# A row maximum on one core: the first block's store moved behind the loads, the load lists retuned, and the last row loaded and reduced in two chained halves

## Chip, cores, metric

One Trainium2 chip, one core of it. The metric is the device time of one execution in microseconds (us); for each kernel the median of several executions is given. The span of a profile is about 1.8 us shorter than the device time of the same execution.

## The reference

```python
x = randn(32, 512, 1024) as float32       # 16384 rows of 1024
return np.max(x, axis=-1)                 # (32, 512) float32
```

Flattened, there are 16384 rows, 128 for each of the 128 partitions. "A row" below means one row in every partition: 128 x 1024 elements, 512 KB. The kernel handles 128 of them.

## The kernel before

Loads go out on the sync queue into a ring of 46 rows; VectorE reduces each load in one instruction. Loads shrink towards the end, so that little is left to reduce once the last one lands. The results leave in two stores on the scalar queue, one for each block: 112 rows (57 KB) and 16 rows (8 KB).

```python
BLOCKS = [
    [14, 14, 12, 11, 9, 8, 8, 7, 6, 5, 4, 4, 4, 3, 3],
    [2, 2, 2, 2, 2, 1, 1, 1, 1, 1, 1],
]
RING = 46
# ... (cut: views of x and out, pools)
    at = first = 0
    for loads in BLOCKS:
        S = sum(loads)
        xb = xf[first * P:(first + S) * P, :].rearrange("(p i) d -> p i d", p=P)
        b = 0
        for g in loads:
            if at + g > RING:
                at = 0
            xc = ring[:, at:at + g, :]
            nc.sync.dma_start(out=xc, in_=xb[:, b:b + g, :])
            nc.vector.reduce_max(out=res[:, first + b:first + b + g], in_=xc, axis=X)
            at += g
            b += g
        dst = bass.AP(tensor=of.tensor, offset=of.offset + first * P, ap=[[S, P], [1, S]])
        nc.scalar.dma_start(out=dst, in_=res[:, first:first + S])
        first += S
```

## Time and profile before

| | before |
|---|---|
| median (range) | 165.06 us (165.01 to 165.14) |
| span of the profile | 163.32 us |
| VectorE (DVE) busy | 138.5 us, 85% |
| load queue's packets, share of the 16 DMA engines | 96.4% |
| first load landed, last load landed | 20.09, 159.46 |
| last reduction | 159.67 to 160.88 |
| small store, issue to landing | 160.91 to 162.33 |
| end | 163.32 |

Times in the lower four rows are from the span's start. A load or store has "landed" when the last of its sixteen semaphore increments is in the trace. The chain, the waits and the windows of this profile stand in the prediction.

### The profile page before, as it was taken

The numbers are of one execution on the slowest core, as the hardware profiler recorded it, in microseconds if no ns is written. First come the engines' busy times: TensorE is split into PE (matmuls) and PEld (weight loads), VectorE is DVE, ScalarE is ACT, GpSimd is POOL, SyncE is SP. The second block draws the span as 40 slices with busy tenths as digits, with TensorE's granted clock in tenths as the row PEclk, the third lists the DMA queues.
The fourth block names the chain that finished last, engine by engine and source line by source line (L and its number), as shares of the span: only waits on it lengthen the run. The fifth ranks groups of instructions, "written<-read, shape, count | busy, mean of one in ns | idle before, by whom it ended". The sixth has DMA issues, their size and how long they took to land.

```text
span 163.3 us, 109 instructions
## 1 busy us (share of the span) xinstructions
DVE 138.5 (85%) x26; POOL 0.2 (0%) x4
## 2 busy tenths in 40 slices
DVE  0000099969999999999999999999999999999994
POOL 0000000000000000000000000000000000000000
DMA  6999999998899897999989999999999999999980
GB/s 225 449 449 449 449 449 449 449 417 385 385 409 522 353 530 321 433 433 441 473 385 473 425 449 400 434 395 451 413 425 433 429 414 418 425 421 419 404 357 2
DMA packets 4032, 67.18 MB, mean 411 GB/s; under 512 B 704, under 2 KB 704, under 8 KB 1472
## 3 DMA queue, kind: packets, MB, share of 16 engines
q1 hardware_dynamic: 3744, 67.11, 96.4%
q10 hardware_dynamic: 288, 0.07, 0.2%
HBM read 67.11 MB, written 0.07 MB: 411 GB/s over the span
## 4 chain that ended last, share of the span: by engine, by line
DMA 57%; DVE 40%; DVEq 1%; SPq 0%; issue 0%
DMA ring<-in_x_dram 57%; DVE res L50 40%; DVEq L82 1%; SPq L49 0%
## 5 line engine op out<-in xcount | busy, mean ns | idle before, releaser
L50 DVE TENSOR_REDUCE res<-ring 128x1 f32<-128x1024 f32 (+11 forms) x26 | 138.5, 5396 | 22.4 <-DMA ring<-in_x_dram 22.4
L71 POOL MEMSET const-bfloat16-1.0<- 128x1 bf16 x1 | 0.1, 101 | 0.0
L71 POOL MEMSET const-uint8-127<- 128x1 uint8 x1 | 0.1, 101 | 0.0
L71 POOL MEMSET const-float32-0.0<- 128x1 f32 x1 | 0.1, 98 | 0.2 <-issue 0.2
L71 POOL MEMSET const-float32-1.0<- 128x1 f32 x1 | 0.1, 98 | 0.0
## 6 DMA issues: line engine op xcount, KB each, us to landing
ring<-in_x_dram SPq DMA_DIRECT2D x2, 7168.0 KB, 27.6
ring<-in_x_dram SPq DMA_DIRECT2D x2, 4096.0 KB, 31.6
ring<-in_x_dram SPq DMA_DIRECT2D x1, 6144.0 KB, 49.9
ring<-in_x_dram SPq DMA_DIRECT2D x3, 2048.0 KB, 36.8
ring<-in_x_dram SPq DMA_DIRECT2D x1, 5632.0 KB, 29.7
ring<-in_x_dram SPq DMA_DIRECT2D x5, 1024.0 KB, 24.6
ring<-in_x_dram SPq DMA_DIRECT2D x1, 4608.0 KB, 23.7
ring<-in_x_dram SPq DMA_DIRECT2D x1, 3584.0 KB, 38.4
```

The source lines that it names most:

```text
L50: nc.vector.reduce_max(out=res[:, first + b:first + b + g], in_=xc, axis=X)
L71: nc = _bacc.Bacc("TRN2", target_bir_lowering=False, num_devices=1)
L82: with _tile.TileContext(nc) as tc:
```

## The change

The intent: keep the 57 KB store out of the way of the loads, and have less to reduce after the last landing, by cutting the last row in two. The first half's maximum is written into the element just in front of the second half, so that the second reduction, over 513 elements, takes it in. The load lists are retuned, the ring gives up one row. The intent is read from the code.

```diff
-    [14, 14, 12, 11, 9, 8, 8, 7, 6, 5, 4, 4, 4, 3, 3],
-    [2, 2, 2, 2, 2, 1, 1, 1, 1, 1, 1],
+    [14, 13, 12, 11, 9, 8, 8, 7, 6, 5, 5, 4, 4, 3, 3],
+    [2, 2, 2, 1, 1, 1, 1, 1, 1, 1, 1, 1],
-RING = 46
+RING = 45
     # ... (cut: `H`, `PAD` and the tile `tail`; the loop is as before, but does not store; `reduce` is its last reduction)
-        nc.scalar.dma_start(out=dst, in_=res[:, first:first + S])
+    half = ring[:, at, :H]
+    nc.sync.dma_start(out=half, in_=xb[:, b, :H])
+    nc.sync.dma_start(out=tail[:, PAD:], in_=xb[:, b, H:])
+    nc.vector.reduce_max(out=tail[:, PAD - 1:PAD], in_=half, axis=X)
+    nc.vector.reduce_max(out=res[:, I - 1:], in_=tail[:, PAD - 1:], axis=X)
+
+    store = nc.scalar.dma_start(out=views[0][0], in_=views[0][1])
+    tc.add_manual_dep(store.ins, reduce.ins.name, SYNC, reason="behind the loads")
+    nc.scalar.dma_start(out=views[1][0], in_=views[1][1])
```

More of the change, by code (lines that the diff above doesn't have):

```diff
@@ L13 @@
 BLOCKS = [
-    [14, 14, 12, 11, 9, 8, 8, 7, 6, 5, 4, 4, 4, 3, 3],
-    [2, 2, 2, 2, 2, 1, 1, 1, 1, 1, 1],
-]
-RING = 46
+    [14, 13, 12, 11, 9, 8, 8, 7, 6, 5, 5, 4, 4, 3, 3],
+    [2, 2, 2, 1, 1, 1, 1, 1, 1, 1, 1, 1],
+]
+RING = 45
+SYNC = mybir.DependencyInfo(mybir.DependencyClass.Sync, mybir.DependencyReason.DATA)
 @with_exitstack
@@ L32 @@
     N, D = xf.shape
+    H = D // 2
     I = N // P
@@ L38 @@
     res = once.tile([P, I], F32)
+    PAD = 16
+    tail = once.tile([P, PAD + H], F32)
     at = first = 0
+    views = []
     for loads in BLOCKS:
-        S = sum(loads)
+        S = sum(loads) + (loads is BLOCKS[-1])
         xb = xf[first * P:(first + S) * P, :].rearrange("(p i) d -> p i d", p=P)
+        dst = bass.AP(tensor=of.tensor, offset=of.offset + first * P, ap=[[S, P], [1, S]])
+        views.append((dst, res[:, first:first + S]))
         b = 0
-        for g in loads:
-            if at + g > RING:
+        for n in loads:
+            if at + n > RING:
                 at = 0
-            xc = ring[:, at:at + g, :]
-            nc.sync.dma_start(out=xc, in_=xb[:, b:b + g, :])
-            nc.vector.reduce_max(out=res[:, first + b:first + b + g], in_=xc, axis=X)
-            at += g
-            b += g
-        dst = bass.AP(tensor=of.tensor, offset=of.offset + first * P, ap=[[S, P], [1, S]])
-        nc.scalar.dma_start(out=dst, in_=res[:, first:first + S])
+            xc = ring[:, at:at + n, :]
+            nc.sync.dma_start(out=xc, in_=xb[:, b:b + n, :])
+            reduce = nc.vector.reduce_max(out=res[:, first + b:first + b + n], in_=xc, axis=X)
+            at += n
+            b += n
         first += S
     assert first == I
+    if at + 1 > RING:
+        at = 0
+    half = ring[:, at, :H]
[6 more added lines that the diff above has]
+    nc.scalar.dma_start(out=views[1][0], in_=views[1][1])
 _INS = ['x']
```

## The prediction

> **What bounds the kernel now.** I read the page first: VectorE (DVE) is 85% busy, the load queue's packets take 96.4% of the DMA engines' time. Neither is clearly the bound, so I went to the chain that ended last, in order of time:
>
> ```profile
> 0.73 0.37 SPq L49
> 1.15 35.88 DMA ring<-in_x_dram
> 37.05 58.02 DVE res L50 x5
> 95.08 36.77 DMA ring<-in_x_dram
> 131.87 19.94 DMA ring<-in_x_dram
> 151.84 7.92 DVE res L50 x6
> 159.75 1.13 DVEq L82
> ```
>
> Columns: start, length, what. The loads carry the end up to 151.81 us; from there seven reductions run back to back, x6 plus the last one (1.13 us, shown under the exit). Then comes the small store, issued at 160.91, and the exit at 163.3.
>
> The waits say how close the two streams are:
>
> ```profile
> DVE res L50 <- DMA ring<-in_x_dram: 22.4, 4, 20.1
> ...
> SPq L49 <- DVE res L50: 77.6, 7, 15.1
> SPq L49 <- DMA ring<-in_x_dram: 56.5, 10, 18.0
> ...
> SPq L49 <- DMA out_dram<-res: 5.0, 1, 5.0
> ```
>
> Columns: total us, times, longest. DVE waits only four times, 20.1 us of it for the first load. The sync queue's long waits look alarming but harm nothing if the DMA engines never run dry. I tested that with the windows view, cut at the moments (the trace's semaphore increments) when one load had landed and the next began to count:
>
> ```profile
> 131.85:135.55 3.70, 3.70 (x2) 0.00 (x0) 1.00 1.01 425
> ...
> 144.21:146.70 2.49, 2.49 (x2) 0.00 (x0) 1.00 1.02 424
> 146.70:149.33 2.63, 2.63 (x2) 0.00 (x0) 1.00 1.02 421
> 149.33:151.81 2.48, 2.31 (x2) 0.00 (x0) 1.00 0.99 413
> 151.81:153.09 1.28, 1.25 (x1) 0.00 (x0) 1.00 1.02 406
> ```
>
> The sixth column is the share of DMA engines busy, about 1.0 up to the last load, as in every earlier stretch. So landings are spaced by transfer alone: 16.94 us for 14 rows (20.09 to 37.03), 14.53 for 12, 9.71 for 8, 4.90 for 4, 3.69 for 3, 2.49 for 2, 1.28 for 1. A line through these is **1.2045 us per row plus 0.08 us per load**. One interval is off: 2.63 in place of 2.49, exactly where the 57 KB store's packets run (146.4 to 149.0). The store costs the load stream 0.14 us. The last load lands at 159.46.
>
> VectorE is a little faster per row:
>
> ```profile
> L50 DVE TENSOR_REDUCE res<-ring 128x14 f32<-128x14336 f32 x2 | 30.2, 15086 | 22.0 <-DMA ring<-in_x_dram 22.0
> L50 DVE TENSOR_REDUCE res<-ring 128x8 f32<-128x8192 f32 x2 | 17.4, 8681 | 0.2 <-DMA ring<-in_x_dram 0.2
> ...
> L50 DVE TENSOR_REDUCE res<-ring 128x2 f32<-128x2048 f32 x5 | 11.2, 2279 | 0.2 <-DMA ring<-in_x_dram 0.2
> ...
> L50 DVE TENSOR_REDUCE res<-ring 128x1 f32<-128x1024 f32 x6 | 6.8, 1208 | 0.0
> ```
>
> From 2279 and 1208 ns one row costs 1.07 us. Starts of back-to-back reductions are closer than the durations, since one begins about 0.08 us before the other ends: 1.127 us for 1 row, 2.194 for 2, 3.26 for 3, 4.327 for 4, 5.393 for 5. Thus a row costs 1.067 and an instruction 0.06. The two streams run nearly level: DVE works off the backlog of a big load over the shrinking ones. At the end it is still behind: the last load is complete at 159.46 and its reduction starts at 159.67.
>
> **What the Trainium skill says.** "DMA: Bandwidth & Descriptors", section "Specifications", gives a fabric ceiling of 435 GB/s; my slope is 524,288 B / 1.2045 us = 435 GB/s, so the trace agrees and the loads cannot go faster per byte. The same page, "Issuing engines are not separate DMA queues", says that DMAs of all issuers interleave on the same 16 engines; the 2.63 us interval is that. "VectorE: DVE Perf Modes", section "The perf-mode tier table", gives tensor_reduce only the 1x mode; 1.067 us per 1024 elements (0.96 per ns) agrees, so there is no quicker form. The same page, "The DRAIN you can't avoid", says a same-engine read-after-write needs its semaphore: the chained halves pay one exposed completion. The trace before has no such pair, so I estimate it.
>
> **The change, part by part.** I used the landings above and the two start-to-start rules. A reduction starts at the later of its landing (plus 0.02) and its predecessor's slot.
>
> 1. *Load sizes.* The first 13 loads hold 106 rows in both kernels (before 14,14,12,11,9,8,8,7,6,5,4,4,4; after 14,13,12,11,9,8,8,7,6,5,5,4,4). So load 13 lands at the same 131.85. The ring shrinks by a row, yet each load is still issued with others in flight: load 4 waits for the first reduction (35.2) while loads 2 and 3 last until 50.4; load 6 waits for the third (63.3) while load 5 lasts to 74.6. A reuse wait for the completion of the load eight back is also early: the last half may go at 150.5, nine us before it lands. No starvation.
>
> 2. *Load stream at the end.* 22 rows remain in both. Before: 13 loads and the store's 0.14. After: 16 loads (two halves), no store among them. Three loads more cost 3 x 0.08 = 0.24; the store gives back 0.14. Last landing about 159.46 + 0.10 = 159.56.
>
> 3. *VectorE.* Before, reduction 13 starts at 131.91. After, its predecessor ends its slot at 131.76, so it starts on the landing, 131.87. Then: 4.327 + 2 x 3.26 + 3 x 2.194 + 9 x 1.127 = 27.57, so the first half starts at 159.44, though it has been there since about 158.9. VectorE, not the load, bounds the end. A half of 512 elements lasts 1.208 - 0.533 = 0.675, ending 160.11. The second reads the first's result: it starts only after that, plus 0.03 (the release that the trace shows from VectorE to the scalar queue, 160.879 to 160.912), and lasts 0.676: end 160.82. Before: 160.88. Gain **0.06 us**. Broken up: without the store VectorE would not have stood 0.19 us before the load at 151.81 plus small lag elsewhere (about 0.3 in all); the extra instructions cost about 0.06 each for two splits, and two chained halves cost 0.675 + 0.03 + 0.676 = 1.38 against 1.21 for one row, a loss of 0.17. The halving is a loss where VectorE is late.
>
> 4. *Stores.* The big store is issued at 159.53, once the last whole row is reduced. With no load before it, I take the small store's 1.42 us from issue to landing (160.91 to 162.33) plus a few tenths: lands by 161.5. Its issue occupies the scalar queue 0.38 us, to 159.9. The small store goes at 160.85 and lands at about 162.27. Nothing is added behind.
>
> 5. *Exit.* The sync engine waits for eight completion semaphores in four pairs, in fixed order; in the trace these steps are 0.07 us apart (162.39, 162.46, 162.53) once the first is released. In the built programs the small store's semaphore sits in the first pair before and in the third after. Two steps, 0.13 us, then pass before the landing: gain **0.13 us**.
>
> Sum: 0.06 + 0.13 = 0.19 us. 165.07 - 0.19 = **164.88 us**.
>
> **The rivals.** (a) *The end follows the load, as the change intends*: the second half would start at 159.58 and end at 160.26, for 164.3 us. For: the halves are smaller than a row. Against: the row sums leave VectorE 0.5 us late, and chaining serializes. (b) *The big store lies at the end*: if its short runs of 448 B take as long to land as before (142.87 to 149.51, 6.6 us), the end would be at 166.2 and the time near 168.9, slower by over 2%. For: that number. Against: its packets first ran 3.5 us after issue, behind queued loads, and took 25 ns each, eight per engine; with the queue empty that shrinks to tenths of a us. (c) *Small descriptors cost more than the line says*: 2 KB runs or nine one-row loads slowing the stream by 0.1 each where VectorE catches up: at most 1 us, 165.9. Against: six one-row loads ran at 1.25 to 1.29.
>
> **Range and chances.** Runs spread by 0.13 us. My terms are each below 0.3, their errors mostly independent; about 0.3 us around 164.88, widened downward for (a) and upward for (c) and for another chip: 164.4 to 165.3. A 2% change is 3.3 us, over ten times every gain I find: faster 0.01; slower 0.015, for (b); within 2% 0.975.
>
> **What would show it.** Right: the big store's packets stand after the last load; no 2.63 us interval; last half landed near 159.55; VectorE without a wait after 131.9 and two reductions of 0.68 us separated by about 0.03; small store issued near 160.85; exit shorter by 0.13. Wrong: VectorE waiting for a half (rival a), the exit waiting for the big store (b), or one-row landings spaced over 1.35 us (c). A wait in the chained pair of some tenths rather than 0.03 would put the time level with before.

## The result

| | median | lowest to highest | ratio to before, 95% interval |
|---|---|---|---|
| before, 6 runs | 165.06 us | 165.01 to 165.14 | |
| changed, 6 runs | 165.02 us | 164.87 to 165.17 | 0.9997, 0.9984 to 1.001 |

A ratio here is the mean time of one kernel's fast runs over that of the other's of the same rounds, so not quite the ratio of the medians quoted. The two kernels are the same within 2%, and the interval holds 1. The predicted 164.88 is 0.14 us low; the measured time lies in the predicted range of 164.4 to 165.3.

The profile of the changed kernel was taken of its slowest run (165.17), and its first load landed at 20.29 instead of 20.09: everything in it stands 0.2 us later from the start. Keep that in mind for each time read from it. The chain that ended last, start, length and what:

```profile
63.94 30.30 DMA ring<-in_x_dram
94.24 0.02 issue
94.27 65.48 DVE res L58 x21
159.75 0.60 DVE tail L69
160.35 0.02 issue
160.38 0.69 DVE res L70
```

Before, the loads carried the end up to 151.81. Now the view stays on VectorE from 94.27 on: 21 reductions, then the halves (L69 and L70).

The view shows a wait only where the engine stood idle. Back to back, a reduction starts about 0.08 us before the one in front of it ends, so a late landing can hold VectorE up unseen. Call the earliest start that the predecessor allows the slot; the prediction's start-to-start times give it (1.127 us after the start of a one-row reduction, 4.327 after one of four rows). In the changed kernel the last start that a landing set is that of the 13th reduction: it began at 132.09, on its landing (132.07), where its slot was 127.69 + 4.327 = 132.02. From there on VectorE alone sets the starts: 27.57 us pass to the first half (132.09 to 159.66), exactly the sum that the prediction worked out. But it does not stay far behind the loads. Over the nine single rows, which land every 1.28 us and take 1.127, its lateness shrinks from 1.33 us to 0.09. The windows between landings:

```profile
144.42:146.91 2.49, 2.49 (x2) 0.00 (x0) 1.00 1.00 410
146.91:148.19 1.28, 1.28 (x2) 0.00 (x0) 1.00 1.02 406
...
158.44:159.11 0.67, 0.67 (x2) 0.00 (x0) 1.00 0.65 232
```

Two rows land in 2.49 us, one in 1.28, half a row in 0.67. The interval of 2.63 us, in which the big store ran, is gone. The DMA issues of the big store (KB, us from issue to landing), of the kernel before and then of the changed one:

```profile
out_dram<-res ACTq DMA_DIRECT2D x1, 56.0 KB, 6.6
```

```profile
out_dram<-res ACTq DMA_DIRECT2D x1, 56.0 KB, 1.6
```

It takes 1.6 us where nothing is queued in front of it. The end of the changed kernel in order of time (start, length, engine, line, what):

```profile
159.66 0.68 DVE L69 TENSOR_REDUCE tail<-ring 128x1 f32<-128x512 f32 x1
159.78 0.38 ACTq L73 DMA_DIRECT2D out_dram<-res  x1
160.38 0.69 DVE L70 TENSOR_REDUCE res<-tail 128x1 f32<-128x513 f32 x1
161.10 0.34 ACTq L75 DMA_DIRECT2D out_dram<-res  x1
```

The first half had landed at 159.11 and is taken up at 159.66: VectorE is 0.55 us late. Nearly all of this comes from the last whole row, which landed at 158.44, was taken up at 158.53 and holds its slot for 1.127 us. The second half landed at 159.75 and has to wait until 160.38 for the first's result. So the halves are reduced one after the other, both after their data.

To compare traces whose first load landed at different times, two measures are used below. **A** is the end of the last reduction minus the landing of the first load; it holds all that the load stream and VectorE do. **B** is the end of the span minus the end of the last reduction; it holds the small store and the exit, which is what the engines still do once that store has landed.

| kernel | A | B | median |
|---|---|---|---|
| before | 140.79 | 2.44 | 165.06 |
| changed | 140.77 | 2.33 | 165.02 |

A is unchanged within 0.02 us, B is 0.11 shorter. Over all thirteen traces the first load landed between 19.99 and 20.29; that alone moves a single run by as much as any part of this change.

### The profile page after: what moved, and what is told of

Read it like the earlier page. It is cut to its first block, busy times and chain, and to the rows that moved or that the text cites. A ratio compares the mean times of both kernels' runs of the same rounds, so it can differ in the third digit from the quotient of the medians.

```text
span 163.4 us, 117 instructions
## 1 busy us (share of the span) xinstructions
DVE 139.0 (85%) x29; POOL 0.2 (0%) x4
## 4 chain that ended last, share of the span: by engine, by line
DVE 49%; DMA 48%; SPq 1%; issue 0%
DMA ring<-in_x_dram 48%; DVE res L58 48%; SPq L57 1%; DVE res L70 0%; DVE tail L69 0%
## 5 line engine op out<-in xcount | busy, mean ns | idle before, releaser
L58 DVE TENSOR_REDUCE res<-ring 128x1 f32<-128x1024 f32 (+12 forms) x27 | 137.7, 5165 | 22.1 <-DMA ring<-in_x_dram 22.1
L70 DVE TENSOR_REDUCE res<-tail 128x1 f32<-128x513 f32 x1 | 0.7, 686 | 0.0
L69 DVE TENSOR_REDUCE tail<-ring 128x1 f32<-128x512 f32 x1 | 0.7, 682 | 0.0
```

Of the source, the lines that this page charges most:

```text
L58: reduce = nc.vector.reduce_max(out=res[:, first + b:first + b + n], in_=xc, axis=X)
L69: nc.vector.reduce_max(out=tail[:, PAD - 1:PAD], in_=half, axis=X)
L70: nc.vector.reduce_max(out=res[:, I - 1:], in_=tail[:, PAD - 1:], axis=X)
```

## Experiments

Each ran five times beside nine runs of the kernel before, whose median was 165.08 us (e1 to e4), 165.10 (e5 to e8) and 165.02 (e9 to e11). Each of these three rounds had another chip. All runs are within 2% of the kernel before, and many medians differ by less than the spread of their runs, so most readings below rest on A and B, which come from one trace each. How well A repeats can be seen: 140.77 and 140.74 in two traces of the changed kernel, 140.62, 140.61 and 140.60 in three with the late store and the old loads (e1, e5, e11). The theory: VectorE, not the last load, carries the end; the store's move and the load list gain a little there, the chained halves give it back. The rivals: the store or the halves pay as they were meant to.

### e1: the store's move alone

```diff
 # the kernel before
-        nc.scalar.dma_start(out=dst, in_=res[:, first:first + S])
+        views.append((dst, res[:, first:first + S]))
...
+    store = nc.scalar.dma_start(out=views[0][0], in_=views[0][1])
+    tc.add_manual_dep(store.ins, reduces[-2].ins.name, SYNC, reason="behind the loads")
+    nc.scalar.dma_start(out=views[1][0], in_=views[1][1])
```

> The kernel before with one change: the big store is ordered behind the last reduction but one; loads, ring and last row as before. Theory (VectorE carries the end; the early store delays loads by 0.14 us and makes VectorE stand 0.19 us at 151.8): the 2.63 us landing interval and that wait are gone, last reduction ends near 160.6 (before 160.88), small store still in the first exit pair, so time 165.06 - 0.25 = about 164.8. Rival A (the store costs the end nothing): 165.06. Rival B (the late store is waited for at the end): 165.5 or more.

Measured: 164.93 us (164.84 to 165.11), ratio 0.9992 (0.9978 to 1.0005); A 140.62, that is 0.17 less than before; B 2.43. The interval of the ratio holds 1; e5 and e11, which differ from e1 by four tiny loads at the start, repeat A. VectorE's waits:

```profile
DVE res L53 <- DMA ring<-in_x_dram: 22.4, 3, 20.3
```

The view counts three waits where it counted four: VectorE stands only 0.07 us before the landing at 151.8 us, where it stood 0.19 (0.15 us behind its slot in place of 0.28). The move is worth 0.15 to 0.17 us, somewhat less than the 0.25 expected, since part of the wait stays. The late store is not waited for: it lands at 161.40, the small one at 162.32.

### e2: the changed kernel with the store in its old place

```diff
+        if loads is BLOCKS[0]:
+            nc.scalar.dma_start(out=views[0][0], in_=views[0][1])
...
-    store = nc.scalar.dma_start(out=views[0][0], in_=views[0][1])
-    tc.add_manual_dep(store.ins, reduce.ins.name, SYNC, reason="behind the loads")
```

> The changed kernel with the big store put back to where the first block ends. Theory: the store again takes about 0.14 us from the load stream near 147-150 us, but here VectorE is over 1 us behind its loads at that time, so nothing of it reaches the end: time within 0.1 of the changed kernel, about 165.0. Rival (moving the store is what the change lives from): 0.14 to 0.2 us slower than the changed kernel, about 165.2.

Measured: 165.01 us (164.99 to 165.14), ratio 0.9998 (0.9985 to 1.001); A 140.75, B 2.32. With the new load list the store's place makes next to no difference. The store lengthens one landing interval to 1.38 us (146.72 to 148.10), and VectorE takes up that row at 149.32, 1.22 us late, so the later landing holds nobody up there. But the lateness shrinks with every single row, and the last whole row of e2 starts on its landing (158.33, taken up at 158.35), 0.02 us after its slot: the store has used up the 0.09 us that the changed kernel had left there, and only just does not show in A. The new list and the store's move are two remedies for the same wait. The list's share can be read from e4 below, which has the halves and the early store but the old list: A is 140.94 there and 140.75 here, 0.19 less; the medians, of one round and without overlap (165.35 to 165.49 against 164.99 to 165.14), agree in direction. Each of the two alone gains 0.17 to 0.19, both together (e3) 0.17.

### e3: the changed kernel with the last row whole

```diff
-    nc.sync.dma_start(out=half, in_=xb[:, b, :H])
-    nc.sync.dma_start(out=tail[:, PAD:], in_=xb[:, b, H:])
-    nc.vector.reduce_max(out=tail[:, PAD - 1:PAD], in_=half, axis=X)
-    nc.vector.reduce_max(out=res[:, I - 1:], in_=tail[:, PAD - 1:], axis=X)
+    nc.sync.dma_start(out=row, in_=xb[:, b, :])
+    nc.vector.reduce_max(out=res[:, I - 1:], in_=row, axis=X)
```

> The changed kernel with the last row as one load and one reduction. Theory (VectorE is late, so the chained pair is a loss): last reduction ends 0.2 us earlier from its slot (1.21 in place of 0.68 + 0.04 + 0.69), about 160.65 against 160.85 at equal first landing; the small store's semaphore moves to the second exit pair, which gives back 0.07; time about 0.13 us under the changed kernel, 164.9. Rival (the halves shorten the end, since the end follows the last load): 0.4 to 0.5 us slower than the changed kernel, 165.5.

Measured: 164.94 us (164.87 to 164.99), ratio 0.999 (0.9978 to 1.0003); A 140.62, 0.15 less than the changed kernel; B 2.39, 0.06 more. Undoing the halves does not cost the 0.5 us that they were meant to bring; it gains 0.08 in the median (0.03 against the second measurement of the changed kernel, e10), which the runs alone do not settle. The last reduction:

```profile
159.56 1.22 DVE L68 TENSOR_REDUCE res<-ring 128x1 f32<-128x1024 f32 x1
```

The whole row landed at 159.53, so it starts on its landing: VectorE and the loads arrive together here, and VectorE is late for the halves mainly because the first of them comes so soon after a whole row.

### e4: the halves alone

```diff
 # the kernel before; store early, RING = 45
-    [2, 2, 2, 2, 2, 1, 1, 1, 1, 1, 1],
+    [2, 2, 2, 2, 2, 1, 1, 1, 1, 1],        # and the last row in two chained halves
```

> The kernel before with one change: its last row in two chained halves (and the ring a row smaller to make room); early store and load list as before. Theory: the chained pair costs 1.40 us where one row took 1.21, so last reduction ends near 161.07, exit pair still the first; time about 165.25. Rival (halves pay): end of the last reduction about 0.5 us earlier, time 164.6.

Measured: 165.38 us (165.35 to 165.49), ratio 1.0019 (1.0007 to 1.0032): slower, clear of noise. A 140.94, 0.15 more than before; B 2.49. The end in order of time:

```profile
159.82 0.68 DVE L63 TENSOR_REDUCE tail<-ring 128x1 f32<-128x512 f32 x1
160.53 0.69 DVE L64 TENSOR_REDUCE res<-tail 128x1 f32<-128x513 f32 x1
161.25 0.34 ACTq L66 DMA_DIRECT2D out_dram<-res  x1
```

From 159.82 to 161.22 it is 1.40 us for one row, which takes 1.21 whole. A and B account for 0.20 of the 0.30 in the median. The rest is not settled; in this trace the first load landed at 20.28, before at 20.09, which may be chance.

### e6: the last row in four chained quarters

```diff
-    H = D // 2
+    Q = 4
+    H = D // Q       # (cut: four loads, four reductions, each taking in the last one's maximum)
```

> The changed kernel with the last row in four chained quarters. Theory (each link of the chain costs an exposed completion on VectorE, which is already late): four reductions of about 0.41 us with three gaps of 0.035, 1.75 us in place of 1.41, so the last reduction ends 0.34 later; small store in the fourth exit pair, 0.07 back; time about 0.27 above the changed kernel, 165.3. Rival (smaller last pieces shorten the end): up to 0.3 us below the changed kernel, 164.7.

Measured: 165.21 us (165.18 to 165.24), ratio 1.0008 (0.9995 to 1.0021), 0.19 to 0.24 above the changed kernel; A 141.11, 0.34 more than the changed kernel, as expected; B 2.23, 0.10 less, of which 0.09 is the time from the small store's landing to the end: that store moved to the fourth exit pair. Two of the reductions and the last one:

```profile
159.83 0.88 DVE L73 TENSOR_REDUCE tail<-tail 128x1 f32<-128x257 f32 x2
160.74 0.42 DVE L74 TENSOR_REDUCE res<-tail 128x1 f32<-128x257 f32 x1
```

A quarter of the work takes 0.42 us, a third of a row's 1.21, and 0.035 us stand between one and the next. More links, more loss.

### e7: the changed kernel, with VectorE relieved (wrong result)

```diff
-            reduce = nc.vector.reduce_max(..., in_=xc, axis=X)
+            reduce = nc.vector.reduce_max(..., in_=xc if n > 1 else xc[:, :, :H], axis=X)
```

The loads are all there, but VectorE reads only half of each of the nine single rows.

> WRONG RESULT ON PURPOSE: the changed kernel, but VectorE reads only half of each of the nine single rows, which gives it slack; loads, stores and the chained halves as they are. Theory (the halves would pay only if VectorE were on time): it now waits for each landing, the first half starts on its landing, the second ends 0.75 us after the last landing in place of 1.31: time about 0.55 under the changed kernel, 164.45. Rival (the loads or the stores carry the end anyway): no change, 165.0.

Measured: 164.48 us (164.35 to 164.56), ratio 0.9964 (0.995 to 0.9977); A 140.17, 0.60 less than the changed kernel; B 2.32, the same within 0.01.

```profile
158.16 0.69 DVE L58 TENSOR_REDUCE res<-ring 128x1 f32<-128x512 f32 x1 [0.60 <-DMA ring<-in_x_dram]
158.84 0.69 DVE L69 TENSOR_REDUCE tail<-ring 128x1 f32<-128x512 f32 x1
...
159.56 0.69 DVE L70 TENSOR_REDUCE res<-tail 128x1 f32<-128x513 f32 x1
```

The bracket shows VectorE standing 0.60 us before the half row, so it is on time now. The first half starts at 158.84 (it landed at 158.82), the second ends at 160.25, 0.79 us after the last landing (159.46), where the changed kernel took 1.31. VectorE is shown to carry the end of the changed kernel: nothing else was altered, and the last load landed 139.38 us after the first, as against 139.46 and 139.40 in the two traces of the changed kernel.

### e8: the same relief with the last row whole (wrong result)

```diff
 # e3, and:
-            reduce = nc.vector.reduce_max(..., in_=xc, axis=X)
+            reduce = nc.vector.reduce_max(..., in_=xc if n > 1 else xc[:, :, :H], axis=X)
```

> WRONG RESULT ON PURPOSE: the same slack with the last row whole (e3_whole_row). Theory: the last reduction starts on its landing and ends 1.23 us after it, hardly before e3 (which was 1.25 after), so 164.9; the halves are thus worth 0.45 us where VectorE has slack, against a loss of about 0.15 where it has none. Rival (halves are never worth anything): e7 and e8 equal.

Measured: 164.88 us (164.83 to 164.92), ratio 0.9988 (0.9975 to 1.0); A 140.65, B 2.40.

```profile
159.46 1.22 DVE L68 TENSOR_REDUCE res<-ring 128x1 f32<-128x1024 f32 x1 [0.57 <-DMA ring<-in_x_dram]
```

A whole row starts on its landing and takes its 1.22 us. Against e3 the slack brings nothing (A 140.62 there): a whole row cannot start before it has landed. Against e7 the halves gain 0.40 us in the median and 0.47 in A. They are good for what they were made for, under a condition that the kernel does not meet.

### e9: which slack it takes (wrong result)

```diff
-  in_=xc if n > 1 else xc[:, :, :H]
+  in_=xc if n > 1 or first + b + 2 == I else xc[:, :, :H]      # the last single row is read whole
```

> WRONG RESULT ON PURPOSE: as e7_slack_halves, but the last of the nine single rows is read whole, so VectorE is on time when that row lands and has a full row to do before the halves. Theory (what the halves need is not slack in general but a VectorE that is free when the first half lands, and a whole row just before them, 1.13 us for a row against 0.68 us to the next landing, already denies that): the first half starts about 0.45 late, the second ends about 1.2 us after the last landing, the same as a whole row (1.23), so time about 164.9 as in e8. Rival (any slack in the tail makes the halves pay): about 164.5 as in e7.

Measured: 164.98 us (164.76 to 165.07), ratio 0.9995 (0.9983 to 1.0008); A 140.71, B 2.32.

```profile
158.43 1.22 DVE L58 TENSOR_REDUCE res<-ring 128x1 f32<-128x1024 f32 x1 [0.60 <-DMA ring<-in_x_dram]
159.56 0.68 DVE L69 TENSOR_REDUCE tail<-ring 128x1 f32<-128x512 f32 x1
...
160.28 0.69 DVE L70 TENSOR_REDUCE res<-tail 128x1 f32<-128x513 f32 x1
```

VectorE waits for the row at 158.43, so it is on time. The half lands at 159.07, yet VectorE takes it up at 159.56, when the row's slot is over. The second half ends 1.27 us after the last landing (159.69), no better than the whole row of e8 (1.24). One whole row in front of the halves undoes all of their gain. More slack earlier could not help, since that row already starts on its landing.

### e5 and e11: the late store alone, and another semaphore for the small store

In the trace before, the sync engine leaves its last four waits, each for two semaphores, one after the other, 0.07 us apart; the small store's is in the first. The transfers of these programs share eight completion semaphores in turn. Four tiny loads at the start move the small store's on to the fourth wait.

```diff
 # e1, and:
+    spare = once.tile([1, 64], F32)
+    for i in range(4):
+        nc.scalar.dma_start(out=spare[:, 16 * i:16 * i + 16], in_=xf[0:1, 16 * i:16 * i + 16])
```

> The kernel with the late store alone (e1_store_late) and, at the start, four loads of 64 bytes on the scalar queue that nobody reads; they only move the final store's semaphore from the first exit pair to the fourth. Theory: the exit steps for the other pairs are then passed before the store lands, so span end minus small store's landing falls from 0.99 to about 0.79 us, all else as in e1: 164.93 - 0.20 = about 164.73. Rival (the exit's length is fixed, the difference of 0.12 seen between the traces was chance): 164.93.

Measured in e5: 164.79 us (164.67 to 164.80), ratio 0.998 (0.9968 to 0.9993); A 140.61, as in e1; from the small store's landing to the end 0.81 us, where it was 0.99 in e1 and before. B is 2.28, 0.15 less than in e1; the other 0.03 was lost because the small store took 1.44 us from issue to landing in place of 1.41. The other traces fit: 1.01 with the store in the first pair (e4), 0.94 in the second (e3, e8), 0.88 in the third (changed, e2, e7, e9), 0.79 in the fourth (e6). e10, the changed kernel once more, and e11, e5 once more, ran on one chip:

> The changed kernel itself, beside the others on one chip: 165.0, and last reduction 140.77 us after the first landing as in its first trace.

> The correct kernel of e5_exit_order again (late store, whole rows, final store's semaphore in the fourth exit pair), on the chip of e10_after_again: 164.8, 0.2 us under the changed kernel and 0.3 under the kernel before. If it falls within 0.1 of the changed kernel, its gain was the chip's.

Measured: e10 164.97 us (164.81 to 165.00), ratio 0.9994 (0.998 to 1.0007), A 140.74, B 2.33; e11 164.76 us (164.64 to 165.01), ratio 0.9984 (0.9972 to 0.9997), A 140.60, B 2.28. e11 is a correct kernel. It is 0.26 us under the kernel before, 0.16%; that is far below 2%, but the interval excludes 1 both times (e5 and e11). Its median is 0.21 us under the changed kernel's of the same chip; there the runs overlap (164.64 to 165.01 against 164.81 to 165.00), so the runs alone do not show it, though A and B are together 0.19 less.

## Why the prediction was right

Its range and no change within 2% held. Its gain of 0.19 us did not show in the medians (0.04, and 0.05 in e10). A range of 0.9 us around a kernel that hardly changes would have held for many a wrong account too; what speaks for this one is that its steps are found in the traces:

1. *Load sizes and no starvation*: right. At equal first landing the thirteenth load landed at the same time (131.85 - 20.09 = 111.76 us after the first before, 132.07 - 20.29 = 111.78 in the changed kernel). The share of busy DMA engines was not about 1.0 in every earlier stretch, as the prediction read it: the recorded view has 0.91 for 0 to 10 us and 0.89 for 20 to 30. The landings still fit the line there, 16.94 us for the second load of 14 rows.
2. *Last landing 0.10 later, measured from the first*: 139.38 before, 139.46 in the changed kernel's first trace, 139.40 in e10. Right in direction, and the sizes differ by less than 0.1. The store cost the last landing somewhat more than 0.14: without it 139.18 (e1), so 0.20. The three loads cost 0.22 to 0.28 by these traces, predicted 0.24.
3. *VectorE bounds the end; gain 0.06*: the mechanism is right, and e7 shows it by relieving VectorE. The gain in A was 0.02 in the first trace and 0.05 in e10. Halves of 0.68 and 0.69 us with a gap of 0.035, predicted 0.675, 0.676 and 0.03. Its loss of 0.17 for the halves was 0.15 (e3, e4). Its breakdown does not add up: 0.3 - 2 x 0.06 - 0.17 is 0.01, not the 0.06 that the start times give. The term at fault is "about 0.3 in all" for what VectorE loses to the store: 0.28 is what it stood behind its slot at 151.84, and 0.15 of that stayed in e1 without the store; e1 gave 0.17 in A. The prediction credited the store with the gain; e2 shows that in the changed kernel the load list had already earned it.
4. *Big store by 161.5 and not waited for*: landed at 161.39.
5. *Exit 0.13 shorter*: 0.99 to 0.88, so 0.11; e5 confirms the reason.

The sum of A and B is 0.13 less, the medians differ by 0.04 (and by 0.05 in e10). In e10 A and B are 0.17 less. The remaining 0.09 to 0.12 is within what single runs vary by, of which the first landing is a visible part; what sets that is open.

Of the rivals, (a), the end following the load, fell: it would have needed what e7 had to fake, and there it came out at 164.48, near the 164.3 that the prediction gave it. What the prediction did not see is that (a) was out of reach of the kernel's shape: e9 shows that slack before the last whole row does not help while that row stands before the halves. The 0.5 us of lateness that the prediction worked out (0.55 measured) are that row's 1.127 us less the 0.67 us until the half lands, plus 0.09. (b), the big store at the end, did not come: 1.6 us instead of 6.6. (c), slow small loads, did not come either: 1.28 us for a row, 0.64 to 0.67 for a half.

Where the intended gain went: the halves lost 0.15 us on a VectorE that was late, and the store's move and the list together earned 0.17: that is A, unchanged. The place of the small store's semaphore, a by-product of the number of transfers, gave 0.11 in B. Both are smaller than the spread of the runs.

## What to carry to other kernels

Cutting the last piece pays only if the engine that consumes it is free when the first part lands; compare the time of the piece just before it (1.13 us) with the time until the next landing (0.67), not totals. Two remedies for the same wait did not add up here (0.17 and 0.19 us alone, 0.17 together): test each with the other in place. In a kernel tuned to a tenth of a microsecond, look also at the order of the waits after the last store, which a count of transfers can shift.

## What the Trainium skill lacked or had wrong

- "DMA: Bandwidth & Descriptors", section "Measured (HBM→SBUF, 128 partitions, SWDGE, issued from GpSimd)", rates a 1 MB transfer at 78% of peak and advises at least 1 MiB. These are transfers issued from GpSimd; the loads here were issued from the sync queue, with others always in flight, and a 512 KB load landed every 1.28 us against 1.2045 by the slope, 94%: an extra load cost 0.08 us. The conditions differ, so this does not refute the page; it has no figure for loads of 512 KB and less queued behind each other.
- "VectorE: DVE Perf Modes", section "The DRAIN you can't avoid", measures eight tensor_copy with a semaphore after each as no slower than with one after the last, and says that the semaphore costs nothing extra there. For a reduction that waits for the one before it and reads its result, something is lost here: in the changed kernel the halves start 0.717 us apart (159.660 to 160.377), while two half-row reductions that do not depend on each other start 0.593 apart (149.229 to 149.822 in e7; 0.594 in e8 and e9), so a link costs about 0.12 us. The page has no figure for this case.
- None of the pages that the prediction drew on tells what the order of the exit's waits costs: about 1.0, 0.94, 0.88 or 0.8 us from the last landing to the end, by the place of the last store's semaphore.
